# A quarter moved into the gated scan's weights, S5's powers taken jointly, and half of the memory's keys moved ahead of the merge

## The chip, the cores and the metric

The kernel runs on one core of a Trainium2 chip (trn2). The metric is the device time of one execution, in microseconds (us). A core has a matrix engine (TensorE, PE in the profile, with its weight loads shown as PEld), VectorE (DVE), ScalarE (ACT), GpSimd (POOL) and SyncE (SP), each with its own queue of instructions, and DMA engines that move weights from memory. An engine works through its queue in order, and waits where an instruction's data or buffer is not there.

## What is computed

The reference is a trunk of two decoder layers on 256 rows of 1024 channels, all in float32:

```
for l in range(DEPTH):
    h = rmsnorm(x, norm_mix[l])
    (u_ssm, q_lat, kv_lat, k_rope, hg_q, hg_f, hg_i, hg_g, gate_logits) = split(h @ w_in[l])
    y_ssm = s5_mixer(u_ssm, ...)     # diagonal complex scan, gelu, z_out * sigmoid(z_gate), [z_out, z_gate] = y @ w_glu
    y_mla = mla_mixer(q_lat, kv_lat, k_rope, ...)        # 8 causal heads
    y_hg  = hgrn2_mixer(hg_q, hg_f, hg_i, hg_g, lower_bounds[l], ...)  # gated linear recurrence, normed, gated, @ w_o
    gates = sigmoid(gate_logits).reshape(b, s, 3, 1024)
    merged = gates[..., 0, :] * y_ssm + gates[..., 1, :] * y_mla + gates[..., 2, :] * y_hg
    x = x + merged @ w_out[l]
    x = x + memory_cross_attention(rmsnorm(x, norm_cross[l]), rmsnorm(mem, norm_mem[l]), ...)  # k, v = split(mem @ w_kv)
    x = x + swiglu_ffn(rmsnorm(x, norm_ffn[l]), ...)
return rmsnorm(x, norm_final)
```

## The kernel before

**Weights.** All weight matrices stream once from memory. A `Chunk` is one transfer or two into one of `RB` = 3 raw buffers of 1 MB (tile `raw`), and is cut into units of up to 1024 columns. ScalarE copies a unit into a rounded high part `wH` (`acopy`, L232), and VectorE takes the rest, `wL` = raw - `wH` (`tt`, L221); there are `HU` = 4 buffers for each. PE multiplies three times per tile (all through `mm`, L213): high by high and high by low of the activations, and low by high. In `projA` (tiles `hv`, `quad`, `acc`, `dn`) that is one matmul of 512 columns with `wH` and one of 256 with `wL`; in `projB` (`gt`, `ho`, `mo`, `zg`, `zo`) it is three of 512.

**Stages of a layer.** The norm and the input projection (`quad`, `acc`, `hv`, then the gate logits `gt`, which give the gates `Tg`); beside these run tasks: S5 (`s5_powers`, `s5_main`), the recurrence `hgrn`, the attention `mla_attn` and the memory's norm `memory`. Then come the output projections of the three mixers (`ho`, `mo`, and `zg`, `zo` in `scan`), the merge's transposes (`mT`, split into `m`), `w_out` (`quad`, `hv`), cross attention and the FFN (`hv`, `dn`).

**S5.** `s5_powers` makes the operators: B times the powers 0 to 3 of the decay `lam` (`Q`), and C times its powers 0 to 4 (`Pw`, `P4`). `s5_main` works on two halves of 16 groups each: ScalarE masks `Q` into `Gp` and `Pw` into `Cp`, PE makes the scan's inputs (`gt<-ident,Gp`, `tm`, `b`), VectorE rotates (`w`), scans (`rt`), and rotates back into `X`, one for each of the real and the imaginary part; PE then forms `y` from `Cp` with `X` and from `Tm` with `Ush`.

**hgrn's output.** The squares of `o` are summed on PE (`oc<-ones,osq`), VectorE scales, GpSimd takes the power -1/2 (`s<-s,mhalf`, L250), PE spreads the result over the partitions (`ro<-ident,s`), VectorE multiplies (`osb<-osb,ro`), and the split gives `hox` for `ho`.

**The merge.** `scan(i)` handles half `i` of the output columns. `zg` is the gate of S5's output, `zo` its value; VectorE computes (tanh(zg/2)+1)*(g+1)/4*zo with g the tanh form of the merge gate, adds it to the accumulator `Tg` and PE transposes (`mT`). The sigmoids' factors are those quarters.

**The start.** `first(k)` feeds the first projection (`quad`) with `h` while ScalarE squares and GpSimd adds (`sq<-sq,sq`, L659; `fold`, L577) for the norm; `hg_bounds` computes the recurrence's lower bounds from `hg_lb` with small VectorE operations (`s`, 128x4).

**What sets the order.** The Python program emits the main line of projections, and `pace()` interleaves the tasks' steps with it by estimated engine times. SBUF tiles get slots from `plan` (class `Plan`, `SLOTS`), and the framework's scheduler then orders each engine's instructions by its own estimates, except where `tc.keep_in_program_order` pins one. Small edits so move instructions far from them.

## Time and profile before

| | us |
|---|---|
| runs before | 1093.49, 1093.5, 1094.94 |
| median of them | 1093.5 |
| the profiled execution's own time | 1094.6 |
| its span, first to last instruction | 1092.8 |
| PE busy in it | 1072.5 |
| VectorE busy | 829.1 |
| ScalarE busy | 636.4 |
| GpSimd busy | 37.7 |

The profiled execution is 1.1 us above the median. The busy time of an engine counts its instructions on data; PE's matmuls overlap, so that its rows can be longer than the distance to the next row. The mean granted clock of PE over the span is 0.992 of 2.4 GHz.

### The profile page before, as it was taken

The page shows a single profiled execution, that of the slowest core. Times are in us where ns is not written, and L with a number is a line of the kernel's source. Part 1 is how long each engine was busy: PE and PEld are TensorE (multiplying, and loading weights), DVE is VectorE, ACT ScalarE, POOL GpSimd, SP SyncE. Part 2 cuts the span into 40 slices and gives each one's busy share as a digit, 9 for nine tenths or more (in the row PEclk, how much of TensorE's full clock was granted, in tenths as well). Part 3 has the DMA queues.
Part 4 walks back from the last instruction along what each step waited for, and adds up shares of the span by engine and source line. Part 5 has one row for each costly group of instructions (what it writes and reads, how often), then busy time and mean ns, then how long its engine had stood idle before and what let it go on. Part 6 is the DMA issues. An engine that isn't in the chain of part 4 may idle for free.

```text
span 1092.8 us, 16654 instructions
## 1 busy us (share of the span) xinstructions
PE 1072.5 (98%) x6416; PEld 938.0 (86%) x6416; DVE 829.1 (76%) x1438; ACT 636.4 (58%) x1050; POOL 37.7 (3%) x52
## 2 busy tenths in 40 slices
PE   8999999989899999999999999999999999999997
PEld 8999888878688888888888899888888888888887
DVE  7996777786687789986768887767677868887753
ACT  6645756855455566564565447965545566555542
POOL 4001000000000000000010001000000000000000
PEclk9999999989899999999999999999999999999999
DMA  8745552342655455655656442543474535655551
GB/s 292 214 117 178 176 163 82 116 148 85 204 167 181 133 195 193 193 183 183 188 181 186 121 136 78 191 130 108 163 233 148 197 123 167 194 191 193 174 190 61
DMA packets 145024, 179.08 MB, mean 164 GB/s; under 512 B 13553, under 2 KB 108657, under 8 KB 144945
## 3 DMA queue, kind: packets, MB, share of 16 engines
q1 hardware_dynamic: 144512, 177.45, 50.6%
q8 instruction: 50, 0.82, 0.3%
q10 hardware_dynamic: 432, 0.57, 0.2%
q14 instruction: 30, 0.24, 0.1%
HBM read 174.59 MB, written 1.05 MB: 161 GB/s over the span
## 4 chain that ended last, share of the span: by engine, by line
PE 72%; ACT 1%; DVE 0%; issue 0%; POOLq 0%; POOL 0%; ACTq 0%
PE hv L213 32%; PE dn L213 11%; PE quad L213 6%; PE gt L213 6%; PE xv L213 2%; PE ho L213 1%; PE mo L213 1%; PE lv L213 1%; PE vps L213 1%; PE zg L213 1%; PE y L213 1%; PE zo L213 1%; PE xo L213 1%; PE b L213 1%; PE xS L213 1%; PE q L213 1%
## 5 line engine op out<-in xcount | busy, mean ns | idle before, releaser
L232 ACT ACTIVATE wH<-raw 128x1024 fp32r<-128x1024 f32 (+2 forms) x332 | 340.7, 1032 | 312.7 <-PE hv L213 81.3
L221 DVE TENSOR_TENSOR wL<-raw,wH 128x1024 fp32r<-128x1024 f32 (+2 forms) x332 | 394.8, 1192 | 158.2 <-ACT wH L232 152.1
L213 PE MATMUL hv<-h,wH 128*128 128x512 f32 x848 | 298.2, 396 | 0.0
L213 PE MATMUL hv<-h,wL 128*128 128x256 f32 x848 | 236.8, 282 | 0.0
L213 PEld LDWEIGHTS hv<-h,wH 128*128 128x128 f32 x848 | 158.6, 188 | 35.3 <-issue 0.2
L213 PEld LDWEIGHTS hv<-h,wL 128*128 128x128 f32 x848 | 160.4, 189 | 1.0
L213 PE MATMUL gt<-wH,h 128*128 128x512 f32 x384 | 123.6, 402 | 0.0
L213 PEld LDWEIGHTS gt<-wH,h 128*128 128x128 f32 x384 | 70.7, 188 | 13.4
L213 PE MATMUL gt<-wL,h 128*128 128x512 f32 x192 | 75.2, 397 | 0.2 <-DVE wL L221 0.2
L213 PE MATMUL dn<-dx,wH 128*128 128x512 f32 x176 | 61.6, 394 | 0.0
L213 PE MATMUL dn<-wH,dx 128*128 128x256 f32 (+1 forms) x264 | 58.7, 319 | 0.0
L213 PE MATMUL acc<-h,wH 128*128 128x256 f32 x288 | 52.5, 284 | 0.0
L213 PE MATMUL dn<-dx,wL 128*128 128x256 f32 x176 | 49.3, 280 | 0.0
L213 PEld LDWEIGHTS dn<-wH,dx 128*128 128x128 f32 x264 | 43.6, 189 | 4.0
L213 PE MATMUL quad<-h,wH 128*128 128x512 f32 (+1 forms) x160 | 44.6, 359 | 0.5 <-ACT wH L232 0.5
L213 PEld LDWEIGHTS acc<-h,wH 128*128 128x128 f32 x288 | 44.9, 192 | 0.1
L213 PEld LDWEIGHTS gt<-wL,h 128*128 128x128 f32 x192 | 35.9, 188 | 7.5 <-DVE wL L221 0.3
L213 PE MATMUL dn<-wL,dx 128*128 128x256 f32 (+1 forms) x132 | 41.9, 319 | 0.0
L213 PE MATMUL acc<-h,wL 128*128 128x256 f32 x144 | 40.8, 284 | 0.2 <-DVE wL L221 0.2
L213 PEld LDWEIGHTS dn<-dx,wH 128*128 128x128 f32 x176 | 33.1, 188 | 7.7
L213 PE MATMUL quad<-h,wL 128*128 128x256 f32 x128 | 33.8, 292 | 2.3 <-DVE wL L221 2.1
L213 PEld LDWEIGHTS dn<-dx,wL 128*128 128x128 f32 x176 | 33.1, 188 | 0.0
(375 smaller groups left out, 2017.4 us busy)
## 6 DMA issues: line engine op xcount, KB each, us to landing
raw<-in_w_in_dram SPq DMA_DIRECT2D x48, 1024.0 KB, 5.2
raw<-in_ffn_w_gate_up_dram SPq DMA_DIRECT2D x40, 1024.0 KB, 5.1
raw<-in_ffn_w_down_dram SPq DMA_DIRECT2D x17, 1024.0 KB, 5.2
raw<-in_ssm_w_glu_dram SPq DMA_DIRECT2D x16, 512.0 KB, 3.9
raw<-in_w_out_dram SPq DMA_DIRECT2D x8, 1024.0 KB, 7.3
raw<-in_x_w_kv_dram SPq DMA_DIRECT2D x8, 1024.0 KB, 5.1
raw<-in_ffn_w_down_dram SPq DMA_DIRECT2D x6, 768.0 KB, 4.8
raw<-in_hg_w_o_dram SPq DMA_DIRECT2D x4, 1024.0 KB, 5.1
```

Source lines behind the costliest of these rows:

```text
L213: return PE.matmul(o, l, r, start=start, stop=stop)
L221: DVE.tensor_tensor(out=o, in0=a, in1=b, op=op)
L232: return ACT.activation(out=o, in_=a, func=f, **kw)
```

## The change

Five edits. **(1)** In each layer the weights of `zg` and `zo` come as four chunks of 1 MB (rows of `w_glu` by two tiles, the gate's and the value's 512 columns behind one another) in place of eight of 512 KB, and their split multiplies by 0.25: ScalarE's copy by its scale, VectorE by a scalar_tensor_tensor (L217) in place of the tensor_tensor. The tanh of `zg` then needs no scale and VectorE's scaling of the gate, `ts(g_, g_, 0.25, 0.25, ...)`, falls away; (g+1)*zo and (u2+1)*that are two scalar_tensor_tensor. **(2)** `s5_powers` keeps `Q` and `Pw` in one tile `Z` of nine slots for each part, so that one power of both is one operation on 512 columns, where there were two on 256; the conjugate comes in through a sign (`sg_`). **(3)** `keys(0)`, half of the memory's keys (32 `hv<-ex` matmuls, with their chunk of `x_w_kv`), is emitted in `scan(1)` between the last `zo` and the transposes; before, all 64 stood behind `w_out`. **(4)** The column sums of the first norm (`ms`) are pinned between two steps of the first projection. **(5)** The first operation of `hg_bounds` is pinned to its place in the program.

```diff
-SLOTS = dict(t4=23, t2=10, t1=4, tn=8, tk=8, ps=8)
+SLOTS = dict(t9=2, t4=19, t2=10, t1=4, tn=8, tk=8, ps=8)
...
                 self.alloc(c.nk, h)
-                split(self.H, self.L, c.raw[:, :, h * j:h * j + h])
+                v = c.raw[:, :, h * j:h * j + h]
+                if c.quarter:
+                    acopy(self.H, v, scale=0.25)
+                    stt(self.L, v, 0.25, f(self.H), ALU.mult, ALU.subtract)
+                else:
+                    split(self.H, self.L, v)
...
                     for k in (0, 2):
-                        for n, c0 in (("zg", 1024), ("zo", 0)):
-                            C[n, i, k] = wcols(A["ssm_w_glu"][l], k, 2, c0 + 512 * i, 512, "one")
+                        C[part, i, k] = Chunk([wap(A["ssm_w_glu"][l], k, 2, c0 + 512 * i, 512) for c0 in (1024, 0)], 2, 1024)
+                        C[part, i, k].quarter = True
...
+        C["xk"] = [wcols(A["x_w_kv"][l], 0, 8, 0, 256)]
         C["wo"] = [wcols(A["w_out"][l], 4 * i, 4, 0, 512, "row") for i in range(2)]
         C["wo"] += [wcols(A["w_out"][l], 0, 8, 256 * i, 256) for i in range(2, 4)]
-        C["xk"] = [wcols(A["x_w_kv"][l], 0, 8, 256 * i, 256) for i in range(2)]
+        C["xk"].append(wcols(A["x_w_kv"][l], 0, 8, 256, 256))
...
             if j == 3:
                 fold(sq0[0], POOL)
+                nrm.sums = col_sums(sq0[0][:, 0], pin=True)
...
-        tt(lmx, gcol[:, lo:lo + 4], gcol[:, lo + 4:lo + 8], ALU.max)
+        tc.keep_in_program_order(tt(lmx, gcol[:, lo:lo + 4], gcol[:, lo + 4:lo + 8], ALU.max))
...
+        Z = [plan.tile(g, "t9", [128, 9, 16, 16], F32, nm("Z")) for n in range(2)]
+        S5Q[l] = Z
+        sg_ = tn([2, 16])
+        acopy(sg_[:, 0], lam[:, 1, ls])
+        acopy(sg_[:, 1], lam[:, 1, ls], scale=-1.0)
...
+        def cmul(o, a0, a1, b):
+
+            cm = [t2([512], F32, "cm")[:, 0:256 * o[0].shape[1]].rearrange("p (s i h) -> p s i h", i=16, h=16) for _ in range(4)]
+            tt(cm[0], a0, b[0], ALU.mult)
+            tt(cm[1], a1, b[1], ALU.mult)
+            tt(o[0], cm[0], cm[1], ALU.subtract)
+            tt(cm[2], a0, b[1], ALU.mult)
+            tt(cm[3], a1, b[0], ALU.mult)
+            tt(o[1], cm[2], cm[3], ALU.add)
...
+        cmul([z_[:, 3:4] for z_ in Z], bc(coef[:, 0, ls]), bc(coef[:, 1, ls]), [b_.unsqueeze(1) for b_ in B])
         yield
+        lr = lam[:, 0, ls].unsqueeze(1).unsqueeze(3).to_broadcast([128, 2, 16, 16])
         for k in range(1, 4):
-            cmul([q[:, 3 - k] for q in Q], lam, [q[:, 4 - k] for q in Q])
-            yield
...
-        for d in range(1, 5):
-            cmul([q[:, d] for q in Pw] if d < 4 else P4, lam, [q[:, d - 1] for q in Pw], conj=True)
-            yield
+            cmul([z_[:, 3 - k:5 + k:1 + 2 * k] for z_ in Z], lr, bc(sg_, 2), [z_[:, 4 - k:4 + k:2 * k - 1] for z_ in Z])
+            yield
+        cmul([z_[:, 8:9] for z_ in Z], bc(lam[:, 0, ls]), bc(sg_[:, 1]), [z_[:, 7:8] for z_ in Z])
...
-                    acopy(Cp[n][:, :, 0:3, g2, :].rearrange("p i k h -> p k i h"), Pw[n][:, 1:4, i0:i0 + 8, :], scale=gm[g2])
-                    acopy(Cp[n][:, :, 3, g2, :], P4[n][:, i0:i0 + 8, :], scale=gm[g2])
+                    acopy(Cp[n][:, :, :, g2, :].rearrange("p i k h -> p k i h"), Z[n][:, 5:9, i0:i0 + 8, :], scale=gm[g2])
...
-                act(u2[tt_], zg[tt_], AF.Tanh, scale=0.25)
-                g_ = Tg["s", i][:, tt_]
-                ts(g_, g_, 0.25, 0.25, ALU.mult, ALU.add)
-                stt(u2[tt_], u2[tt_], 1.0, g_, ALU.add, ALU.mult)
+                act(u2[tt_], zg[tt_], AF.Tanh)
             half("zo", zo, 2)
+            if i == 1:
+                drain()
+                keys(0)
             tps = [bank("mT") for _ in range(2)]
             for tt_ in range(2):
                 acc = Tg["h", i][:, tt_]
-                tt(u2[tt_], u2[tt_], zo[tt_], ALU.mult)
+                g_ = Tg["s", i][:, tt_]
+                stt(g_, g_, 1.0, zo[tt_], ALU.add, ALU.mult)
+                stt(u2[tt_], u2[tt_], 1.0, g_, ALU.add, ALU.mult)
                 tt(acc, acc, u2[tt_], ALU.add)
...
         drain()
-        Kc = t4([4, 256], F32, "Kc")
-        Rm = t1([256], F32, "Rm")
-        row_of(rmc, Rm)
-        for i in range(2):
-            kc = Kc[:, 2 * i:2 * i + 2]
-            add_up(kc, halves(C["xk"][i], ex))
-            tt(kc, kc, Rm.unsqueeze(1).to_broadcast([128, 2, 256]), ALU.mult)
+        keys(1)
```

The order of the instructions moves at places far from these lines too. VectorE's queue in the second half of S5 of layer 0, ahead of the first `X` (`w` are the rotated inputs, `cs` and `sn` cosine and sine, `rt` the scan's decay): before,

```order
L931 SCALAR_TENSOR_TENSOR w_2531<-rt_2346,w_2529 128x512
L221 TENSOR_TENSOR wL_2572<-raw_2279,wH_2571 128x1024
L221 TENSOR_TENSOR w_2528<-cs_2345,w_2530 128x8x63
L221 TENSOR_TENSOR s_2556<-s_2552,lsc_1283 128x2
L221 TENSOR_TENSOR w_2529<-sn_2344,w_2531 128x8x63
L228 TENSOR_SCALAR Tg_2596<-Tg_2596 128x512
L221 TENSOR_TENSOR wL_2732<-raw_2279,wH_2731 128x1024
L221 TENSOR_TENSOR X_2613<-w_2528,w_2529 128x8x63
```

and with the change:

```order
L937 SCALAR_TENSOR_TENSOR w_2445<-rt_2280,w_2443 128x512
L217 SCALAR_TENSOR_TENSOR ex_2859<-mT_2813,gcol,ex_2859 128x256
L221 TENSOR_TENSOR w_2443<-sn_2278,w_2445 128x8x63
L217 SCALAR_TENSOR_TENSOR ex_2859<-mT_2813,gcol,ex_2859 128x256
L217 SCALAR_TENSOR_TENSOR ex_2942<-mT_2813,gcol,ex_2942 128x256
L221 TENSOR_TENSOR X_2543<-w_2442,w_2443 128x8x63
```

Splits and gate scalings stood between the second scan and `X`; now three operations of the memory's norm (`ex`) stand there. A third split, before this excerpt, is gone from between `b` and `X` as well.

PE's queue at the end of the merge of layer 0: before,

```order
L213 MATMUL zo_2938<-wH_2941,yx_2701 128x512
L213 MATMUL zo_2938<-wL_2942,yx_2701 128x512
L1415 MATMUL mT_3024<-ident,Tg_1712 128x128 x2
L1415 MATMUL mT_3025<-ident,Tg_1712 128x128 x2
L213 MATMUL quad_3056<-m_1500,wH_2959 128x512
L213 MATMUL quad_3056<-m_1500,wL_2960 128x256
```

and with the change, from the last of the keys' matmuls on:

```order
L213 MATMUL hv_2983<-ex_2977,wH_2929 128x512
L213 MATMUL hv_2983<-ex_2977,wL_2930 128x256
L1420 MATMUL mT_3038<-ident,Tg_1675 128x128 x2
L213 MATMUL quad_3069<-m_1487,wH_2954 128x512
L213 MATMUL quad_3069<-m_1487,wL_2955 128x256
```

The transposes of the second half (`mT_3024` before, `mT_3038` now) followed the last `zo` directly. Now four `hv<-ex`, the eight transposes of the first half that remained, and 28 `hv<-ex` stand between.

PE's queue at hgrn's output in layer 0: before, behind the sums `oc` and 30 `gt`,

```order
L629 MATMUL ro_2010<-ident,s_1984 128x128 x4
L213 MATMUL gt_1884<-wH_1886,h_117 128x512
L213 MATMUL gt_1884<-wL_1887,h_117 128x512
L213 MATMUL S_2078<-Kh_1294,Qh_1292 128x128
L213 MATMUL gt_1885<-wL_1887,h_117 128x512
L213 MATMUL y_2166<-Tm_1904,Ush_333 64x4x32
L213 MATMUL y_2166<-Cp_2028,X_2062 64x4x32
```

and with the change, from the end of `y` on:

```order
L213 MATMUL y_1994<-Cp_1928,X_1949 64x4x32
L213 MATMUL oc_2019<-ones,osq_1963 128x1 x8
L213 MATMUL gt_1887<-wH_1888,h_117 128x512 x2
L213 MATMUL gt_1887<-wL_1889,h_117 128x512
L213 MATMUL S_2097<-Kh_1281,Qh_1279 128x128
L213 MATMUL S_2097<-Kh_1281,Qh_1279 128x256
L637 MATMUL ro_2065<-ident,s_2030 128x128 x4
L637 MATMUL ro_2083<-ident,s_2030 128x128 x4
L979 MATMUL yt_2054<-ident,ysh_2041 128x128 x4
L213 MATMUL S_2193<-Kh_1281,Qh_1279 128x128
L213 MATMUL S_2193<-Kh_1281,Qh_1279 128x256
L213 MATMUL ho_2091<-wH_1923,hox_2064 128x512
```

S5's `y` stood behind `ro`; now `oc`, `ro` and `ho` come behind `y`, close to one another.

## Rows read from the trace of the kernel before

**Rows 1.** The page, busy time and share of the span of an engine.

```profile
PE 1072.5 (98%) x6416; PEld 938.0 (86%) x6416; DVE 829.1 (76%) x1438; ACT 636.4 (58%) x1050; POOL 37.7 (3%) x52
```

**Rows 2.** Busy time by engine in stretches of 25 us, granted clock, DMA.

```profile
50.00:75.00 25.00, 25.00 (x182) 23.57 (x181) 24.97 (x75) 12.63 (x15) 0.00 (x0) 1.00 0.52 159
225.00:250.00 25.00, 21.15 (x122) 17.63 (x121) 20.11 (x43) 13.91 (x33) 0.92 (x3) 0.86 0.36 117
275.00:300.00 25.00, 21.18 (x97) 17.13 (x96) 15.87 (x24) 10.35 (x17) 0.00 (x0) 0.86 0.62 207
```

**Rows 3.** Timeline of PE: start, duration, instruction, idle time ahead and its releaser.

```profile
238.14 0.57 PE L213 MATMUL y<-Cp,X 128*64 128x128 f32 x2 [2.49 <-DVE X L221]
239.02 0.47 PE L1094 MATMUL PT<-ident,Ssb 128*128 128x128 f32 x1 [0.31 <-ACT Ssb L232]
240.55 0.69 PE L1094 MATMUL PT<-ident,Ssb 128*128 128x128 f32 x2 [1.05 <-DVE Ssb L226]
...
287.99 0.66 PE L1415 MATMUL mT<-ident,Tg 128*128 128x128 f32 x4 [2.36 <-DVE Tg L221]
...
290.81 0.77 PE L213 MATMUL quad<-m,wH 128*128 128x512 f32 x1 [1.46 <-DVE m L221]
```

**Rows 4.** Stretches of 1 us behind those pauses; the clock is third from the end.

```profile
244.00:245.00 1.00, 1.00 (x8) 1.00 (x9) 0.00 (x0) 1.00 (x5) 0.00 (x0) 0.50 0.00 0
295.00:296.00 1.00, 1.00 (x4) 0.81 (x4) 0.00 (x0) 0.00 (x0) 0.00 (x0) 0.50 0.01 1
```

**Rows 5.** Timeline of PE, ends of the two stretches at the lower clock.

```profile
241.17 0.69 PE L213 MATMUL y<-Cp,X 128*64 128x128 f32 x2
...
245.06 0.64 PE L213 MATMUL y<-Cp,X 128*64 128x128 f32 x6
...
296.52 0.40 PE L213 MATMUL quad<-m,wH 128*128 128x512 f32 x1
...
296.87 0.40 PE L213 MATMUL quad<-m,wH 128*128 128x512 f32 x1
```

**Rows 6.** Timelines of GpSimd, VectorE and PE, where GpSimd adds.

```profile
8.81 1.58 POOL L659 TENSOR_TENSOR sq<-sq,sq 128x512 f32<-128x512 f32 x1 [5.29 <-ACT sq L232]
...
91.86 0.74 POOL L577 TENSOR_TENSOR sqq<-sqq 128x256 f32<-128x256 f32 x1
...
9.13 1.28 DVE L221 TENSOR_TENSOR s<-s 128x4 f32<-128x4 f32 x1
...
91.90 1.24 DVE L221 TENSOR_TENSOR wL<-raw,wH 128x512 fp32r<-128x512 f32 x1 [0.89 <-ACT wH L232]
...
14.87 0.74 PE L213 MATMUL quad<-h,wL 128*128 128x256 f32 x4 [2.11 <-DVE wL L221]
```

**Rows 7.** Groups of VectorE's instructions: busy us and mean ns, idle before.

```profile
L221 DVE TENSOR_TENSOR wL<-raw,wH 128x1024 fp32r<-128x1024 f32 (+2 forms) x332 | 394.8, 1192 | 158.2 <-ACT wH L232 152.1
...
L221 DVE TENSOR_TENSOR cm<-lam,Pw 128x256 f32<-128x256 f32 x32 | 12.3, 419 | 0.1
...
L217 DVE SCALAR_TENSOR_TENSOR mu<-mu,Tg 128x512 f32<-128x512 f32 x8 | 5.5, 687 | 0.4 <-ACT mu L232 0.4
...
L228 DVE TENSOR_SCALAR Tg<-Tg 128x512 f32<-128x512 f32 x8 | 3.4, 423 | 1.6 <-ACT Tg L232 1.6
```

**Rows 8.** Timelines of GpSimd, PE and VectorE at hgrn's output (678.01 is layer 1).

```profile
170.22 2.48 POOL L250 TENSOR_TENSOR s<-s,mhalf 128x8 f32<-128x8 f32 x1 [5.14 <-DVE s L228]
...
678.01 1.64 POOL L250 TENSOR_TENSOR s<-s,mhalf 128x8 f32<-128x8 f32 x1 [13.54 <-DVE s L228]
...
175.86 1.03 PE L629 MATMUL ro<-ident,s 128*128 128x128 f32 x8
...
178.26 1.28 DVE L221 TENSOR_TENSOR osb<-osb,ro 128x512 f32<-128x512 f32 x2
...
181.58 1.28 DVE L221 TENSOR_TENSOR hox<-osb,hox 128x512 fp32r<-128x512 f32 x2
```

**Rows 9.** Timeline of PE behind the start.

```profile
29.99 0.39 PE L213 MATMUL acc<-h,wL 128*128 128x256 f32 x1 [0.23 <-DVE wL L221]
```

**Rows 10.** The page, DMA issues: KB each, median us from issue to landing.

```profile
raw<-in_w_out_dram SPq DMA_DIRECT2D x8, 1024.0 KB, 7.3
```

## What I predicted

> **What bounds the kernel now.** The page's first block says that TensorE (PE) is busy for 98% of the span [rows 1], so the time can fall by little more than PE's pauses, 20 us in all, and by work that PE does at its lower clock. I read PE in slices of 25 us. Nearly all slices are full of PE work, like 50 to 75 us; three are not: the first one (the start, before weights are there), 225 to 250 and 275 to 300 us, which hold 21.2 us each at a mean clock of 0.86 [rows 2]. The timeline of PE shows what stops it there. At 238.14 the S5 outputs `y` wait 2.49 us for VectorE's (DVE's) `X`, and at 240.55 the softmax transposes wait 1.05 for `Ssb`; a pause of 0.31 lies between. At 287.99 the merge's transposes `mT` wait 2.36 us for DVE's `Tg`, and at 290.81 `quad` waits 1.46 for `m` [rows 3]. Behind each pair of pauses the granted clock is 0.50, the 1.2 GHz level [rows 4]. From 241.17 to 245.06 the `y` matmuls [rows 5] run without a pause at that level, so about half of 3.9 us, 1.9, is lost. From 290.81 to 296.52 nine pairs of `quad` take 5.7 us; at full clock the next pair takes 0.35, nine would take 3.2, so 2.5 is lost [rows 3, 5]. Layer 1 has the same two places and no pause worth counting, so I expect nothing from it.
>
> **S5, second half of layer 0.** The wait at 238.14 is DVE's queue. Ahead of `X` stood three splits `wL` of 1.2 us each and two `Tg` scalings of 0.42 [rows 7]; the order of the change has none of these five between `b` and `X` and three `ex` operations on half as many columns instead, some 0.4 each: 4.4 us out, 1.2 in, so 3 us earlier. PE's cover grows too: 37 `gt` matmuls stand between the last `b` and the first `y`<-`X`, where 21 stood, at 0.23 each (512 of the 768 columns of a `quad` pair's 0.35) 3.7 us more. The wait was 2.5, so it goes, with margin: -3.85 (2.49 + 0.31 + 1.05) and, as the clock does not fall, -1.9. Sum **-5.75**. Both ends: nothing won if DVE comes to `b` 4 us late; no more than 5.75 can be won.
>
> **Merge of layer 0.** Before, after the last `zo`, DVE owed a product with `zo`, a sum, a split and the matching work of the other tile before PE could go on. Now 28 `hv<-ex` matmuls (14 pairs of 0.35 [rows 5], 4.9 us) stand between the transposes of the first half and those of the second, and four more ahead. What DVE owes in that time is four fused operations of 0.69 [rows 7], one split of 1.2 and a sum of 0.6 for the first tile; two splits of `m` and the other sum for the second: about 4.2 us for tile 0 and 5.6 for tile 1, needed at 6.5 (4 `hv`, 8 `mT`, 28 `hv`). So both waits (2.36 + 1.46) and the 2.5 of clock go: **-6.3**. Folding 0.25 into the weights costs nothing: ScalarE's copy has a scale anyway, and DVE's split is a scalar_tensor_tensor with as many columns (the group `mu<-mu,Tg` takes 0.69 for 512, as a tensor_tensor does); it removes four `Tg` scalings per layer, 1.7 us of DVE, hidden work elsewhere. The moved `hv` matmuls are the same in number; where they leave (behind `w_out`) 32 remain, and I see no DVE chain there longer than their 5.6 us.
>
> **Powers of S5.** 48 operations of 256 columns per layer become 12 of 256 and 18 of 512. At 0.42 (`cm`) and 0.69 a piece (the nearest row of that size) [rows 7] that is 20.2 against 17.5 us of DVE per layer, some 1 us of ScalarE per half for fewer `Cp` copies, and two small copies more. All of it lies at times when PE has no pause: 0 on the path, and -2.7 us at most if DVE's full stretch around 50 to 75 us had held PE up, which it did not.
>
> **The start.** `hg_bounds` leaves the first 15 us for 27 to 45 us. There its operations on 128x4 took 1.28 us, against some 0.15 elsewhere: the one at 9.13 began during GpSimd's addition of 8.81 (1.58 us) and ended with it [rows 6]. Three such are 3.4 us of DVE ahead of the `wL` for which PE waits 2.11 at 14.87, and there is about 1.3 of low clock behind it. A wait of the same kind meets a large split: `wL` of 128x512 at 91.90 took 1.24 beside GpSimd's fold at 91.86 [rows 6]. So the block belongs to whatever DVE issues while GpSimd adds; `h` or `wL` will stand in the queue instead, and I put the gain at 0 (ends: 0 and 3.4 + 1.3). The Trainium skill, "SBUF — State Buffer", "Who interferes with whom", says that a DVE instruction with two SBUF inputs contends with a GpSimd instruction that reads SBUF, and that issue order decides who blocks, for the whole instruction. By it, too, the start gains nothing; by the naive sum it gains up to 4.7.
>
> **What the change adds.** (a) Behind the start, `row` comes 24 `acc` matmuls later on PE, so the four `Ue` (on 256 columns, some 0.55 each) fall ahead of a split that `acc` needs; PE waited 0.23 for it at 29.99 [rows 9]. By laying the rows end to end I get 1.1, so **+0.9** (0 to 2.2, the four `Ue` in full). (b) The output of the gated scan `hgrn` in layer 0. Before, 30 `gt` matmuls (7 us) stood between the norm sums `oc` and their use `ro`, and `ro` did not wait, at 175.86 [rows 8]. Now `oc` stands behind all of `y`, with three `gt` and two `S` (1.1 us) ahead of `ro`. The chain in between is a small DVE operation and GpSimd's power, which took 2.48 and, in layer 1, 1.64 [rows 8]; with 1.64 PE waits about 1.0. Then `ho` needs `ro` times `osb` on DVE (0.6 each), a copy on ScalarE and the split `hox` (0.6 as well) [rows 8]; DVE has `ysh`, `ph` and a `wL` of 1.2 among them, PE has only `yt` and two `S` as cover: about 1.1 for the high part and 1.7 for the low. Together **+3.8** (0.5 if the power is short and `wL` early; 6 at the slow ends). (c) Both half-clock stretches above followed a pause over 2 us with more behind it; here the pauses are shorter but three, so the lower level costs 0 to 2.4; I take **+1.2**. (d) Four more table loads of ScalarE, 1.28 each, lie around 30 to 36 us on an engine that has pauses there: 0, or up to 2 if a weight copy behind them is late.
>
> **Sum.** -5.75 - 6.3 + 0.9 + 3.8 + 1.2 = -6.15. The profiled execution took 1094.6 (span 1092.8), 1.1 more than the median of 1093.5; from the median the forecast is **1087.3 us**. A measurement of this kernel tells about 0.2%, 2.2 us, from no change.
>
> **Rivals.**
> 1. The new waits at `ho` are covered (ScalarE's copy and DVE's split come while `ho` still has other weights) or the start does gain. Without (b) and (c) the time is 1082.3; with 2 of the start's 4.7 as well 1080.3. For it: before, `hox` and `ho` ran without a pause. Against it: the few matmuls between `oc`, `ro` and `ho`. Chance 0.28.
> 2. One of the two old pauses stays, because DVE reaches `b` or the last `zo` later than I laid it out: 5.75 or 6.3 come back, 1093.3. For it: I place DVE's start by PE's pace, and 2 us decide at the merge. Against it: at S5 chain and cover move the same way. Chance 0.15.
> 3. Slower: weights arrive late. The gate's weights now come as four chunks of 1 MB, each holding one of three raw buffers until both units are split, and the keys' chunk stands ahead of `w_out`. PE spends 24 matmuls, 5.6 us, on such a chunk; `w_out` took 7.3 us to land [rows 10]. If all four and the keys' chunk land at 7.9 apart, five waits of 2.3 make 11.5 and eat all that is won (11.2 net of (a)); at 8.5 the result is 3 to 4 us slower than before, 1097. Against it: two raw buffers ahead of use give over 10 us of lead, and the stretch 275 to 300 moved 207 GB/s, 5 us per MB [rows 2]. Chance 0.07.
> 4. The change does not do what it says, in that the added order only moves the waits by equal amounts (S5's into `hgrn`'s output, the merge's into `m`): within 2 us of 1093.5. Chance 0.07.
>
> My own case has 0.43, with a range of 1084.5 to 1090. To hold 8 in 10 the range goes from **1080.5** (rival 1 with part of the start) to **1093** (rival 2 in most of its width). Faster by over 0.2% is below 1091.3: all of my case and rival 1, a sixth of rival 2 and some of the others, without a little of my case's slow tail: 0.75. Within 0.2%: 0.17. Slower: 0.08.
>
> **What the profile after would show.** Right: no PE pause over 0.5 us ahead of the first `y`<-`X` of the second half and of `mT`; a clock of 1.00 in both stretches; at `ro` and `ho` of layer 0, around 175 to 185 us, pauses of 1 to 4 us in sum, ended by POOL or DVE; PE's busy time down by 2 to 4 us; the pause at 14.87 still near 2 us, with another DVE operation drawn out beside GpSimd. Wrong: a pause over 2 us at `X`, `Tg` or `m`; PE waiting on a DMA between `zg` and `quad`; or a new half-clock stretch that is longer than both old ones.

## The result, and the profile after

The changed kernel took 1080.28 us (median of four runs, 1080.19 to 1080.35), the kernel before 1093.95 beside it (1093.49 to 1094.94): 0.9874 of it, 95% interval 0.9857 to 0.9891. That is 13.7 us, more than twice the 6.15 that were forecast, and 0.2 us below the low end of the range. The profiled execution took 1080.19 (span 1078.4, 14.4 less than before's 1092.8), at a mean granted clock of 0.998.

The page's lines that answer to [rows 1] and [rows 10]: busy time of each engine, and one row of its DMA issues.

```profile
PE 1063.5 (99%) x6416; PEld 932.8 (86%) x6416; DVE 823.9 (76%) x1394; ACT 639.7 (59%) x1042; POOL 37.6 (3%) x52
...
raw<-in_w_out_dram SPq DMA_DIRECT2D x8, 1024.0 KB, 5.2
```

PE has the same 6416 matmuls and is busy for 9.0 us less, where 2 to 4 were forecast. Some 7.4 of that are matmuls that had run at the lower clock in this profile of before: 1.4 at the start, 3.5 at S5, 2.5 at the merge, worked out further down. `w_out` lands in 5.2 us, not 7.3.

Two of the stretches of 25 us of [rows 2], after:

```profile
225.00:250.00 25.00, 25.00 (x150) 21.22 (x150) 20.90 (x38) 15.24 (x30) 0.22 (x2) 1.00 0.48 146
275.00:300.00 25.00, 25.00 (x143) 21.70 (x142) 19.64 (x33) 13.86 (x22) 0.00 (x0) 1.00 0.57 187
```

Both of them, which stood out before, are now full, 25.00 against 21.15 and 21.18, at a clock of 1.00 against 0.86.

The timeline of the kernel after, at the places of [rows 3, 6, 8, 9] (start, duration, engine, instruction; in brackets the idle time ahead of it and what ended it):

```profile
8.53 1.36 POOL L667 TENSOR_TENSOR sq<-sq,sq 128x512 f32<-128x512 f32 x1 [5.01 <-ACT sq L232]
10.44 1.54 POOL L667 TENSOR_TENSOR sq<-sq,sq 128x512 f32<-128x512 f32 x1 [0.55 <-ACT sq L232]
12.28 1.74 POOL L667 TENSOR_TENSOR sq<-sq,sq 128x512 f32<-128x512 f32 x1 [0.29 <-ACT sq L232]
...
7.85 0.88 DVE L217 SCALAR_TENSOR_TENSOR h<-xp,gcol,h 128x256 fp32r<-128x256 f32 x2
10.36 1.91 DVE L217 SCALAR_TENSOR_TENSOR h<-xp,gcol,h 128x256 fp32r<-128x256 f32 x2
12.80 2.38 DVE L217 SCALAR_TENSOR_TENSOR h<-xp,gcol,h 128x256 fp32r<-128x256 f32 x2
...
12.93 0.74 PE L213 MATMUL quad<-h,wL 128*128 128x256 f32 x4 [0.73 <-DVE wL L221]
15.83 0.74 PE L213 MATMUL quad<-h,wL 128*128 128x256 f32 x4 [1.21 <-DVE wL L221]
28.67 0.38 PE L213 MATMUL acc<-h,wL 128*128 128x256 f32 x1 [1.15 <-DVE wL L221]
113.74 0.70 PE L213 MATMUL rope<-qraw,cf 128*128 128x256 f32 x2 [1.75 <-ACT qraw L232]
...
181.47 1.64 POOL L250 TENSOR_TENSOR s<-s,mhalf 128x8 f32<-128x8 f32 x1 [24.23 <-DVE s L228]
...
181.05 0.71 PE L213 MATMUL gt<-wH,h 128*128 128x512 f32 x2
...
181.82 0.82 PE L213 MATMUL S<-Kh,Qh 96*128 96x128 f32 x4
183.16 1.97 PE L637 MATMUL ro<-ident,s 128*128 128x128 f32 x8 [0.51 <-POOL s L250]
186.41 0.95 PE L213 MATMUL S<-Kh,Qh 96*128 96x128 f32 x4 [0.42 <-DVE osb L221]
188.81 0.50 PE L213 MATMUL ho<-wH,hox 128*128 128x512 f32 x1 [0.51 <-DVE hox L221]
...
234.85 0.68 DVE L221 TENSOR_TENSOR X<-w,w 128x504 f32<-128x504 f32 x1
238.10 0.38 PE L213 MATMUL y<-Cp,X 128*64 128x128 f32 x2
...
284.26 0.68 DVE L221 TENSOR_TENSOR Tg<-Tg,mu 128x512 f32<-128x512 f32 x1
286.36 0.38 PE L1420 MATMUL mT<-ident,Tg 128*128 128x128 f32 x2
```

**The two old waits are gone with margin.** `X` is done at 235.53, and the `y` that had waited 2.49 us for it starts at 238.10. The second `Tg` is done at 284.94, and its `mT`, which had waited 2.36, starts at 286.36. **The start:** PE's pauses there are 0.73 and 1.21, together 1.94, beside 2.11 before. While GpSimd adds, two `h` take 1.91 and 2.38 us, where two take 0.88 ahead of it. **hgrn's output:** 0.51, 0.42 and 0.51. **New:** 1.75 at `rope`, which no step of the prediction named. All pauses of PE's timeline make 13.85 before and 8.60 after. The "20 us in all" with which the prediction begins also held the 6.3 us behind PE's last matmul (1086.5 of 1092.8), which are no pause.

The granted clock (third from the end) in stretches of 1 us at hgrn's output, the only place of the kernel after, up to its last matmul, where it falls below 0.97:

```profile
183.00:184.00 1.00, 0.84 (x4) 0.84 (x5) 0.96 (x4) 1.00 (x3) 0.10 (x1) 0.54 0.00 0
184.00:185.00 1.00, 1.00 (x7) 1.00 (x6) 1.00 (x2) 0.56 (x1) 0.00 (x0) 0.50 0.00 0
185.00:186.00 1.00, 0.98 (x5) 0.58 (x3) 1.00 (x4) 0.00 (x0) 0.00 (x0) 0.50 0.00 0
186.00:187.00 1.00, 0.59 (x4) 0.57 (x5) 1.00 (x2) 0.98 (x3) 0.00 (x0) 0.76 0.00 0
```

Before, it fell in 16 to 20, 238 to 245 and 289 to 297.

### The profile page after: what moved, and what is told of

The parts are those of the page before. It is cut to its first block, busy times and chain, and to the rows that moved or that the text cites. A ratio compares the mean times of both kernels' runs of the same rounds, so it can differ in the third digit from the quotient of the medians.

```text
span 1078.4 us, 16592 instructions
## 1 busy us (share of the span) xinstructions
PE 1063.5 (99%) x6416; PEld 932.8 (86%) x6416; DVE 823.9 (76%) x1394; ACT 639.7 (59%) x1042; POOL 37.6 (3%) x52
## 4 chain that ended last, share of the span: by engine, by line
PE 96%; ACT 2%; DVE 1%; DMA 0%; issue 0%; POOLq 0%; POOL 0%; ACTq 0%
PE hv L213 33%; PE gt L213 12%; PE dn L213 11%; PE quad L213 7%; PE acc L213 5%; PE mo L213 2%; PE zo L213 2%; PE zg L213 2%; PE vps L213 2%; PE ho L213 2%; PE lv L213 2%; PE y L213 2%; PE xv L213 2%; PE b L213 1%; PE q L213 1%; PE oT L213 1%
## 5 line engine op out<-in xcount | busy, mean ns | idle before, releaser
L221 DVE TENSOR_TENSOR wL<-raw,wH 128x1024 fp32r<-128x1024 f32 (+2 forms) x316 | 375.2, 1191 | 152.7 <-ACT wH L232 149.1
```

The costliest lines, as they stand in the source:

```text
L221: return DVE.tensor_tensor(out=o, in0=a, in1=b, op=op)
```

## The experiments

Theory A: each edit acts through the pause that the prediction names, so that the sum of the terms holds and only sizes are off. Theory B: something else in the change gave most of it, such as weights that come earlier, the start, or the clock. The runs do one edit alone on the kernel before, then leave one out of the whole, then test single terms. Kernels that were measured together share their runs of before. Those of different groups ran on different chips, so between groups the ratios are compared.

### One edit alone

**e1_keys**, edit (3):

```diff
+            if i == 1:
+                drain()
+                keys(0)
             tps = [bank("mT") for _ in range(2)]
```

> Only the move of half the memory's keys, on the kernel before. PE's queue has 32 hv<-ex between the last zo and the merge's transposes in both layers; S5, hgrn and the start stand as before. Theory A (each edit removes the waits of its own place, and the gains add): both waits at the merge of layer 0 go (2.36 + 1.46) with the 2.5 us of lower clock behind them, layer 1 gives 0.5 to 1 as well; the waits at X in S5 stay: 1093.5 - 6.3 - 0.7 = about 1086.5. Theory B (the merge gains only if DVE's chain is shortened by the quarter too): DVE still owes the product, the sums and a split per tile, so a wait of 1 to 2 us at mT or m stays, with its clock: 1089 to 1091.

1085.87 us (1084.75 to 1087.89), ratio 0.993 [0.991, 0.995]. No pause is left at `mT` and `m`; `X` still waits 2.49. The keys alone remove the merge's waits, as Theory A has it.

**e2_powers**, edit (2), of which one line is shown:

```diff
-            cmul([q[:, 3 - k] for q in Q], lam, [q[:, 4 - k] for q in Q])
+            cmul([z_[:, 3 - k:5 + k:1 + 2 * k] for z_ in Z], lr, bc(sg_, 2), [z_[:, 4 - k:4 + k:2 * k - 1] for z_ in Z])
```

> Only the joint powers of S5, on the kernel before. The order of S5 and hgrn in layer 0 becomes that of the whole change (39 matmuls between the last b and the first y<-Cp,X where 21 stood, 3 between oc and ro where 30 stood). Theory A: all of S5's gain comes from this edit, by the order that it brings and not by the 2.7 us of DVE per layer: 5.75 won at X, 1.5 to 3 lost at ro, ho and in the clock behind, 1 to 2 won in the FFN and layer 1: 1088 to 1090; the two waits at the merge stay. Theory B: the two Tg scalings that the quarter removes are needed too, a wait of 0.5 to 1 stays at X: 1090 to 1092. If the FFN between 390 and 495 us gets 0.7 shorter here, that part belongs to the powers as well.

1090.83 us (1088.04 to 1091.37), ratio 0.9973 [0.9961, 0.9986]. The pause at `X` is gone, and the ones at hgrn's output (0.52, 1.58, 0.21) and at `rope` (1.77) are there: the powers set the order of S5 and hgrn, and bring both the gain and the price. `quad` waits 1.74 and 3.26 for `m`. The mechanism is Theory A's, since no wait is left at `X`; the time is in Theory B's range.

**e3_quarter**, edit (1), scale and chunks:

```diff
+                if c.quarter:
+                    acopy(self.H, v, scale=0.25)
+                    stt(self.L, v, 0.25, f(self.H), ALU.mult, ALU.subtract)
...
+                        C[part, i, k] = Chunk([wap(A["ssm_w_glu"][l], k, 2, c0 + 512 * i, 512) for c0 in (1024, 0)], 2, 1024)
+                        C[part, i, k].quarter = True
```

> Only the quarter in the weights of zg and zo and their chunks of 1 MB, on the kernel before. Two Tg scalings leave DVE's queue ahead of X in the second half of S5 (0.34 each as it steps): X comes 0.7 earlier, the wait there falls from 2.49 to 1.8. At the merge the transposes still follow the last zo directly, and DVE owes four operations of 0.69 and two sums there in place of two and two. Theory A (no cover, no gain): the wait at mT stays 2 to 4 us, total 1092 to 1094. Theory B (the fused form shortens DVE's chain enough): the merge's waits fall by half or more, 1089 to 1091.

1089.01 us (1088.1 to 1090.7), ratio 0.9962 [0.9945, 0.9979]. `X` waits 1.82 instead of 2.49 (0.67 less, near the 0.84 of the two `Tg` scalings that are gone), `mT` 1.10, `m` 1.41. The time is Theory B's, though the merge's waits fell by a third and not by half.

**e4_pins**, edits (4) and (5):

```diff
-        if l == 0:
-            nrm.sums = col_sums(sq0[0][:, 0])
...
+                nrm.sums = col_sums(sq0[0][:, 0], pin=True)
...
+        tc.keep_in_program_order(tt(lmx, gcol[:, lo:lo + 4], gcol[:, lo + 4:lo + 8], ALU.max))
```

> Only the two pins (column sums of the first norm, first operation of the recurrence's bounds), on the kernel before. The start becomes that of the whole change: no 128x4 operation ahead of the first splits, row 24 acc matmuls later. Theory A (the trace of the whole change: quad ends 2.2 earlier, 0.9 lost again at acc): 1092.2, the clock in 16 to 20 us stays at full level, although DVE's operations are drawn out beside GpSimd's additions as before. Theory B (what I forecast: the block only meets another instruction, and the start gives nothing): 1093.5 to 1094.5 with the loss at acc.

1093.05 us (1088.29 to 1095.37), ratio 0.9998 [0.9986, 1.0009]. The start's pauses are 0.70 and 1.22, `acc` waits 1.14: what the pins give at the start, the later `row` takes at `acc`. The time lies between the two theories, and the interval holds no change.

The four medians are 7.5, 2.5, 4.4 and 0.3 below before's 1093.37, 14.7 in sum; the whole has 13.1 in its second measurement (e9_whole). The sums agree to within 2 us, but the single gains are not what the same edits are worth within the whole (see e10 to e12).

### The halves of the quarter

**e5_chunks** has the chunks of 1 MB without the 0.25, **e6_scale** the 0.25 on chunks of 512 KB:

```diff
-                        for n, c0 in (("zg", 1024), ("zo", 0)):
-                            C[n, i, k] = wcols(A["ssm_w_glu"][l], k, 2, c0 + 512 * i, 512, "one")
+                        C[part, i, k] = Chunk([wap(A["ssm_w_glu"][l], k, 2, c0 + 512 * i, 512) for c0 in (1024, 0)], 2, 1024)
```

```diff
-                split(self.H, self.L, c.raw)
+                if c.quarter:
+                    acopy(self.H, c.raw, scale=0.25)
+                    stt(self.L, c.raw, 0.25, f(self.H), ALU.mult, ALU.subtract)
...
-                tt(u2[tt_], u2[tt_], zo[tt_], ALU.mult)
+                g_ = Tg["s", i][:, tt_]
+                stt(g_, g_, 1.0, zo[tt_], ALU.add, ALU.mult)
+                stt(u2[tt_], u2[tt_], 1.0, g_, ALU.add, ALU.mult)
```

> Of the quarter's edit only the chunks: the gate's weights in four chunks of 1 MB, split as before, no 0.25 in them, the Tg scalings stay; on the kernel before. Theory A (lead): with three raw buffers a chunk of 512 KB gives half the lead, and ScalarE's waits on raw<-ssm_w_glu and raw<-w_out around 268 to 282 us (4.5 and 3.9 before, none in the run of the quarter) came from that; they vanish here too, DVE's splits come earlier, mT and m wait about 2.5 in sum where it was 3.8, X stays at 2.49: 1089.5 to 1091. Theory B (the gain of the quarter is DVE's work): the waits stay, 1093.

> Of the quarter's edit only the 0.25 in the weights and the fused DVE form, with the chunks of 512 KB as before. Theory A (lead): ScalarE's DMA waits of 4 us stay, the waits at mT and m stay at 3 to 4, only X falls from 2.49 to 1.8: 1092 to 1093. Theory B (DVE's work): 1089 to 1090, as with the whole edit.

e5_chunks: 1090.14 us (1089.25 to 1091.45), ratio 0.9971 [0.9959, 0.9983]. e6_scale: 1092.6 (1088.77 to 1093.07), ratio 0.9982 [0.9968, 0.9997]. What the chunks do stands on ScalarE. Its timeline in the kernel before, where the gate's weights are split:

```profile
270.55 1.06 ACT L232 ACTIVATE wH<-raw 128x1024 fp32r<-128x1024 f32 x1 [4.48 <-DMA raw<-in_ssm_w_glu_dram]
...
280.34 2.01 ACT L232 ACTIVATE wH<-raw 128x1024 fp32r<-128x1024 f32 x2 [3.87 <-DMA raw<-in_w_out_dram]
```

and in e6_scale, ScalarE and PE:

```profile
269.71 1.06 ACT L232 ACTIVATE wH<-raw 128x1024 fp32r<-128x1024 f32 x1 [4.58 <-DMA raw<-in_ssm_w_glu_dram]
...
276.52 1.06 ACT L232 ACTIVATE wH<-raw 128x1024 fp32r<-128x1024 f32 x1 [2.84 <-DMA raw<-in_ssm_w_glu_dram]
...
280.02 2.01 ACT L232 ACTIVATE wH<-raw 128x1024 fp32r<-128x1024 f32 x2 [2.44 <-DMA raw<-in_w_out_dram]
...
287.78 1.12 PE L1419 MATMUL mT<-ident,Tg 128*128 128x128 f32 x4 [3.10 <-DVE Tg L221]
```

For comparison e4_pins, which also has chunks of 512 KB:

```profile
276.53 1.06 ACT L232 ACTIVATE wH<-raw 128x1024 fp32r<-128x1024 f32 x1 [1.65 <-DMA raw<-in_w_out_dram]
...
284.36 0.66 PE L1416 MATMUL mT<-ident,Tg 128*128 128x128 f32 x4 [0.74 <-DVE Tg L221]
```

In e5_chunks, e3_quarter and the whole ScalarE waits for no DMA there. A raw buffer holds 1 MB, and three are in the ring; a 512 KB chunk takes a whole one, so that the weights on their way are half as much work. The late copies make late splits on DVE, and these stand in the queue ahead of `Tg`: with the scale alone `mT` waits longer (3.10) than before (2.36), with the chunks alone 0.74. How late the weights of the 512 KB chunks are differs between executions: in the profile of e4_pins `w_out` keeps ScalarE waiting for 1.65 instead of 3.87, and `mT` waits 0.74 there too. So the wait at `mT` in a single profile doesn't show what the chunks do on PE. It is shown by ScalarE, which waits for the gate's weights in all six profiles with chunks of 512 KB and in none of the ten with 1 MB, and by the ten runs of e5_chunks at 0.9971. Chunks of 1 MB bring weights earlier, as Theory A has it for e5 and e6. Rival 3 looked at the right place, the arrival of the gate's weights, with the wrong sign.

### Single terms

**e7_no_ms_pin**, the whole with the column sums back at their old place:

```diff
-                nrm.sums = col_sums(sq0[0][:, 0], pin=True)
...
+        if l == 0:
+            nrm.sums = col_sums(sq0[0][:, 0])
```

> The whole change without the pin of the first norm's column sums (the pin of the recurrence's bounds stays). PE's row comes after 2 acc matmuls again, not 24. Theory A (the late row puts four Ue ahead of acc's split): the pause of 1.15 at acc falls to 0.2, so that the time is 0.9 below the whole change, 1079.4; S5 has 48 matmuls of cover where it had 37, no pause there. Theory B (the pin also shields the first projection from a pause): quad ends later by what acc gains, 1080 to 1081.

1083.12 us (1080.41 to 1084.93), ratio 0.9906 [0.9888, 0.9925]: `acc` waits 0.46 instead of 1.15, but `rope` 2.38 and `ho` 1.16. The later `row` costs its 0.7, and yet the kernel with it is 2.9 faster by the medians, and 1.6 by the ratios of this run and e9_whole, whose intervals overlap; both theories missed that. Without the pin the order differs at two places far behind, and this profile has the clock at 0.50 behind its longer pause at `rope` and behind `ro`. The one run of the six at a mean clock of 0.998 took 1080.41, as the whole does, so the difference is in the main lower clock.

**e8_ro_early**, e7_no_ms_pin with S5's `y` of layer 0 held back until hgrn's sums are emitted, to give `ro` its cover:

```diff
+            while l == 0 and hf == 0 and "ro" not in HGD:
+                yield
...
+        HGD.append("ro")
```

> As e7_no_ms_pin, and in layer 0 S5's y of the first half is emitted only when hgrn has emitted its norm sums: PE has oc within the y matmuls, five eighths of them ahead of ro. Theory A (the waits at hgrn's output are the chain oc, DVE, GpSimd, ro without cover): the pause of 0.51 at ro goes, one of 0.5 to 1.5 at ho stays (DVE multiplies, ScalarE copies, no cover), the clock stays at full level more often there: 1 to 2 less than e7, 1077.5 to 1078.5. Theory B (ho's pause takes all of it): same as e7 within 0.5.

1084.87 us (1084.53 to 1086.32), ratio 0.9926 [0.9909, 0.9943]. No pause at `ro`, but 3.04 at `ho`, which waits for `hox`. The wait moved one step along the chain; the chain from `oc` to `ho` is what counts, not `ro`. The time is 1.75 above e7_no_ms_pin, outside both theories.

**e9_whole**, the changed kernel again, with no edit.

> The whole change once more, on the same chip as the next three, because times of one kernel differ between chips by where the clock falls. Pauses as in its first trace: 0.7 and 1.2 at the start, 1.15 at acc, 0.5, 0.4 and 0.5 at hgrn's output, none at X, mT, m: 1079.5 to 1082. If e7_no_ms_pin was slower than this only by its chip, this run lies at 1082 to 1084.

1080.24 us (1080.22 to 1080.38), ratio 0.9891 [0.987, 0.9912]. This profile shows no stretch at the lower clock at hgrn's output. PE's timeline there:

```profile
183.33 1.09 PE L637 MATMUL ro<-ident,s 128*128 128x128 f32 x8 [0.51 <-POOL s L250]
184.71 0.66 PE L979 MATMUL yt<-ident,ysh 128*128 128x128 f32 x4 [0.29 <-DVE ysh L217]
186.58 0.92 PE L213 MATMUL S<-Kh,Qh 96*128 96x128 f32 x4 [1.21 <-DVE osb L221]
188.98 0.50 PE L213 MATMUL ho<-wH,hox 128*128 128x512 f32 x1 [0.56 <-DVE hox L221]
```

The pauses are 2.57 in sum, 1.13 more than the 1.44 of the first profile, and `ro` takes 1.09 instead of 1.97. From the first `vps` (a projection that starts at 45.80 and 45.98 us) to the first `xS` of the cross attention both executions take 281.55 us. PE waited there for GpSimd and VectorE, whose instructions kept their durations (`osb` takes 0.68 at 185.00 in the first profile, where PE's clock is 0.50, and at 185.17 in this one), and in the time of its slower work it would have waited anyway. The run is not on e7_no_ms_pin's chip, so it doesn't settle what that chip does; the medians of before on the two are 1093.7 and 1093.36.

### The whole without one edit

**e10_no_powers**, **e11_no_quarter** and **e12_no_keys**, a few lines of each edit:

```diff
-            cmul([z_[:, 3 - k:5 + k:1 + 2 * k] for z_ in Z], lr, bc(sg_, 2), [z_[:, 4 - k:4 + k:2 * k - 1] for z_ in Z])
+            cmul([q[:, 3 - k] for q in Q], lam, [q[:, 4 - k] for q in Q])
```

```diff
-                        C[part, i, k] = Chunk([wap(A["ssm_w_glu"][l], k, 2, c0 + 512 * i, 512) for c0 in (1024, 0)], 2, 1024)
-                        C[part, i, k].quarter = True
```

```diff
-            if i == 1:
-                drain()
-                keys(0)
```

> The whole change without the joint powers. Theory A (gains of the parts add; the powers alone gave 2.95): 3 slower than the whole. X waits 1.8 to 1.9 in the second half of S5 of layer 0 (the quarter takes the Tg scalings away), Ssb 0.5 and 1.2, and nothing at hgrn's output. Theory B (the powers only exchange S5's pauses for those at hgrn's output): within 1 of the whole.

> The whole change without the quarter and its chunks of 1 MB. Theory A (gains add; the quarter alone gave 4.15): 4 slower than the whole. Theory B (the keys' cover at the merge already hides what the quarter saved there: both act on the same two pauses): ScalarE waits 3 to 4 us for raw<-ssm_w_glu again, but PE does not at mT or m; 0 to 1.5 slower than the whole.

> The whole change without the moved keys. Theory A (gains add; the keys alone gave 7.6): 7 slower than the whole. Theory B (the quarter has taken a part of the same pauses): mT and m wait about 1.1 and 1.4 as with the quarter alone, with the clock behind them: 4 to 5.5 slower than the whole.

| | us (range) | ratio [95%] | above e9_whole |
|---|---|---|---|
| e10_no_powers | 1084.64 (1083.82 to 1085.08) | 0.993 [0.9911, 0.9949] | 4.4 |
| e11_no_quarter | 1082.52 (1081.84 to 1084.24) | 0.9913 [0.9893, 0.9932] | 2.3 |
| e12_no_keys | 1084.53 (1083.23 to 1085.03) | 0.9929 [0.9911, 0.9947] | 4.3 |

PE's timeline in e10_no_powers, second half of S5, layer 0:

```profile
236.33 0.41 PE L213 MATMUL y<-Cp,X 128*64 128x128 f32 x2 [1.82 <-DVE X L221]
237.21 0.47 PE L1103 MATMUL PT<-ident,Ssb 128*128 128x128 f32 x1 [0.48 <-ACT Ssb L232]
238.74 0.69 PE L1103 MATMUL PT<-ident,Ssb 128*128 128x128 f32 x2 [1.05 <-DVE Ssb L226]
```

and in e12_no_keys, at the merge:

```profile
283.54 0.63 PE L213 MATMUL quad<-m,wH 128*128 128x512 f32 x1 [2.58 <-DVE m L221]
```

Each old pause comes back with its edit: without the powers the three at S5 (and none at `ro`, `ho` or `rope`), without the keys one at the merge, with the clock low from 283.8 to 287.2 behind it. Without the quarter `mT` waits 0.89, `mo` 0.59, and ScalarE waits 1.19, 1.93 and 1.69 us for the gate's weights.

So the places are shown, but the gains don't add. Powers, quarter and keys are worth 2.5, 4.4 and 7.5 alone and 4.4, 2.3 and 4.3 when left out of the whole. The keys came out in Theory B's range (the quarter has taken a part of their pauses), the powers above Theory A's 3, the quarter between its two theories. That the single gains made nearly the whole's 13.1 is in part that these differences cancel.

### The start, and the new pause

**e13_qraw**, the whole with a higher priority for the copy that `rope` waits for:

```diff
-            acopy(qraw, pp[:, 0:256])
+            with tc.high_priority(offset=400):
+                acopy(qraw, pp[:, 0:256])
```

> The whole change, with ScalarE's two copies `qraw` given a higher priority, so that in layer 0 the first of them stands ahead of the two `Kh` copies (2.0 us) instead of behind them; downstream, two `S` matmuls move from ahead of `ho` to behind its first four. If the new pause at `rope` (1.75 us at 113.74 in the profile after) is ScalarE's queue and is lost time, it shrinks by most of 1.75, and the time falls by about that from the whole's 1080.3, to 1078.4 to 1079.2, if the moved `S` does not cost as much at `ho` (0.2 each). Rival: the pause is only where PE's lead over the other engines is taken back; then it moves to a later instruction, and the time stays within 0.4 of 1080.3.

1083.05 us (1081.81 to 1086.52), ratio 0.9921 [0.9895, 0.9946]. All four runs are slower than every run of the whole, by 1.4 to 6.3 us, on another chip. ScalarE's and PE's timelines:

```profile
111.23 0.36 ACT L232 ACTIVATE qraw<-qp 128x256 f32<-128x256 f32 x1
111.62 2.00 ACT L232 ACTIVATE Kh<-kraw 32x1024 f32<-32x1024 f32 x2
...
114.27 1.04 ACT L232 ACTIVATE wH<-raw 128x1024 fp32r<-128x1024 f32 x1
...
115.37 0.73 PE L213 MATMUL gt<-wH,h 128*128 128x512 f32 x2 [1.51 <-ACT wH L232]
...
187.10 1.24 PE L213 MATMUL ho<-wH,hox 128*128 128x512 f32 x4 [2.59 <-ACT hox L232]
```

The rival's mechanism holds, its time (within 0.4) doesn't. `rope` no longer waits, but 1.51 us come back at `gt`, which needs the weight copy that stands behind the same `Kh`. What PE waits for is the whole of ScalarE's queue from 107.7 to 115 us (copies of `Gp`, a table load of 1.28, `sn`, `Kh`), and it hardly matters which instruction shows it. At `ho`, which lost the two `S` as cover, the pause is 2.59, where `S` and `ho` had 1.21 and 0.56 in e9. All pauses make 9.49 us, beside 9.43 in e9, so they only moved; the 1.6 us that this profiled execution is longer lie at hgrn's output, with the clock at 0.50 from 188.1 to 191.5. Why the median is 2.8 above the whole's is not shown.

**e14_no_hg_pin**, the whole without edit (5):

```diff
-        tc.keep_in_program_order(tt(lmx, gcol[:, lo:lo + 4], gcol[:, lo + 4:lo + 8], ALU.max))
+        tt(lmx, gcol[:, lo:lo + 4], gcol[:, lo + 4:lo + 8], ALU.max)
```

> The whole change without the pin of `hg_bounds`: its small VectorE operations stand in the start again. If, as the prediction said, GpSimd's block then only falls on them in place of `h` and `wL`, the start's pauses stay near 2 us in sum and the time within 0.7 of the whole's 1080.3. Rival: the pin is what gave the start's 2.2 us in the profiles; then PE comes to the first `acc` about 2 us later and the time is 1081.5 to 1083.

1080.92 us (1080.83 to 1082.76), ratio 0.9895 [0.9878, 0.9911]; 0.7 above the whole by the medians, 0.4 by the ratios. PE's timeline of the start:

```profile
14.80 0.74 PE L213 MATMUL quad<-h,wL 128*128 128x256 f32 x4 [2.10 <-DVE wL L221]
...
29.44 0.39 PE L213 MATMUL acc<-h,wL 128*128 128x256 f32 x1 [1.07 <-DVE wL L221]
```

Its pause is the one of before, 2.10 beside 2.11, and yet PE comes to the first `acc` 1.39 us sooner than before. One stretch of 1 us tells why, first in the kernel before, then in e14_no_hg_pin, then in e1_keys, which has the start of before as well:

```profile
17.00:18.00 1.00, 1.00 (x6) 1.00 (x7) 1.00 (x3) 0.46 (x1) 0.00 (x0) 0.50 1.06 345
```

```profile
17.00:18.00 1.00, 1.00 (x11) 1.00 (x10) 1.00 (x3) 0.48 (x1) 0.00 (x0) 1.00 1.01 353
```

```profile
17.00:18.00 1.00, 1.00 (x7) 1.00 (x6) 1.00 (x3) 0.50 (x1) 0.00 (x0) 0.50 1.02 354
```

At 0.50 PE has 6 matmuls in that microsecond, at 1.00 it has 11. Behind the same pause of 2.1 us the clock fell in some profiles and not in others: of the seven that have the old start it fell in four (before, e1_keys, e5_chunks, e6_scale) and not in e2_powers, e3_quarter and e14. In none of the nine profiles with `hg_bounds` pinned, where the pauses are 0.5 to 0.8 and 1.2, did it fall there. So the pin gave 0.7 to 0.9 without the clock, and in this pair of profiles 1.4 more through it. That the pin prevents the fall is likely by these counts, and not shown.

## Why the prediction was wrong

The profile's difference of 14.4 us by the prediction's terms. A group's time is the distance from one PE row's start to the next, without the pauses, which are counted apart.

| term | forecast | measured | of which pauses |
|---|---|---|---|
| up to 47 us (start, (a)) | +0.9 | -1.3 | +0.7 |
| S5, second half, layer 0 | -5.75 | -7.4 | -3.85 |
| merge of layer 0 | -6.3 | -6.6 | -3.8 |
| hgrn's output, (b) and (c) | +5.0 | +3.25 | +1.2 |
| `rope` | 0 | +1.6 | +1.6 |
| the rest of layer 0 to cross attention | 0 | -1.2 | 0 |
| from there to the end | 0 | -2.7 | -1.1 |
| sum | -6.15 | -14.4 | |

**S5 and the merge: right.** The places, the direction and the pauses came out as forecast (e1, e10 and e12 show which edit does which). The failed size is the clock at S5: the forecast counted 1.9 for the `y` from 241.17 on. The matmuls that ran below full clock from 238 on were `y` (2.20 gained), `PT` (0.78) and `oT` (0.56), 3.5. At the merge 2.5 was forecast for `quad` and 2.54 measured.

**"Together +3.8" and "+1.2" at hgrn's output: mis-sized.** The pauses came where they were put, with 1.44 after and 2.57 in e9 against 3.8. All in all this place cost 3.25, not 5.0. At `ro` 0.51, not 1.0: the GpSimd power took the 1.64 that was assumed, but the three `gt` and the `S` ahead of `ro` cover 1.6 us (181.05 to 182.64), not 1.1. At `S` and `ho` 0.4 and 0.5 in place of 1.1 and 1.7 at `ho`. The clock did fall (to 0.50 for three microseconds), and by e9 that cost nothing net: slower work replaced waiting. Here a term for low clock beside a term for waits in the same microseconds counted the same time twice.

**"I put the gain at 0" for the start: right about the block, wrong about the clock.** The block moved to `h` (1.91 and 2.38 for two, 0.88 without GpSimd). The Trainium skill, "SBUF — State Buffer", section "Who interferes with whom", says that a VectorE instruction with two SBUF inputs contends with a GpSimd instruction that reads SBUF, and that the order of issue decides which of them is blocked; the rows agree. The start's pauses fell by 0.17 only. The pin's 0.7 to 0.9 (e14) stands against the later `row`'s 0.9, and (a) measured 1.15 - 0.23 = 0.92, as forecast. The remaining -1.4 is the clock: the prediction saw "about 1.3 of low clock" behind the old pause and put it at 0 with the rest, and the clock fell in four of seven profiles of the old start and in none of nine of the new one.

**The zeros: wrong.** "Layer 1 has the same two places and no pause worth counting, so I expect nothing from it": its merge is 1.1 us shorter, and its pauses of 0.31 and 0.30 there and of 0.47 at `o` are gone. Keys alone shorten that merge (from its first `zg` to the first `xS`) by 1.4, the scale alone by 1.1, the chunks alone by 0.2. For the powers, "0 on the path": e2 and the whole spend 0.7 to 0.8 us less in layer 0's FFN, where no other edit does. This is no scatter: the FFN's 593 `hv` matmuls take 104.21 us from the first to the last (390.83 to 495.04 before) in each of the seven profiles without the joint powers and 103.50 (379.06 to 482.56 after) in each of the nine with them. PE has no pause there in either; the steps from one matmul to the next are shorter, by 0.2 to 0.3 us in a hundred behind the first 300. The edit changes VectorE's work there (the powers of layer 1) and the slots of the tiles (`SLOTS`); which of the two does it was not tested. The -1.2 in the rest of layer 0 is spread in the same way, over `tm` (0.45), `lv` (0.41), `o` (0.33) and `x` (0.20), and no run singles out its cause. And `rope` is the same zero with the other sign, +1.6: ScalarE's work of S5's first half now stands ahead of `qraw`. It comes with the powers (e2, e9, e11, e12) and is absent without them (e1, e3 to e6, e10).

**The failing steps.** The pauses at the two old places (3.85 and 3.82) went as forecast. Of the 8.2 us that the sum missed in this pair of profiles, 4.2 are its terms for the lower clock: 1.9 at S5 where 3.5 was gained, 0 at the start where 1.4 was, and +1.2 at hgrn's output that cost nothing net. The second failing step is the zeros for the rest of the kernel: 3.9 were gained there (the rest of layer 0, its FFN, layer 1), of which `rope`, another zero, took 1.6 back. The price on the waits of the new order was near: 3.25 for 3.8. The rest are the pin's 0.85 and 0.3 at the merge.

Of the rivals, the first named a time (1080.3 to 1082.3) next to the result. Its conditions came half: the start did gain about 2 in the profiles, 1.4 of it by the clock, but at hgrn's output 3.25 of the 5.0 that it leaves out stayed, and gains that it doesn't name made up for them. That its time is so near is luck in part. The third had chunks of 1 MB make weights late; they made them early, worth some 3 us alone by e5. Its argument counted the bytes that a chunk holds and not the lead that a ring of three gives when each buffer is full.

**What the clock adds.** In 61 runs of the kernel before beside the experiments the time goes with the granted clock: 1088.69 and 1088.70 at 0.998, 1096.06 to 1096.28 at 0.989. All eight runs of the changed kernel have 0.998 or 0.999 and agree within 0.2 us. At equal mean clock the change is thus worth 8.4 us, and some 5 of the 13.7 are lower-clock stretches that the kernel before has in most executions and the changed one has not, or has where they cost nothing. What is open: why the clock falls behind a given pause in one execution and not in the next, and why the matmuls of layer 0's FFN follow one another a little faster.

## What to carry to other kernels

When an order is remade by a scheduler, price the places far from the edit too: here they held +3.25, +1.6 and -3.9 us beside the two pauses that the change removed, and 1.4 us of clock at the start came and went between profiles of the same instructions, so that a gain by the clock has to be counted over several executions. Count PE's low clock only where PE is not waiting for another engine in the same microseconds. Don't add the gains of single edits where two of them act on the same pause. In a ring of few buffers of fixed size, chunks that half fill a buffer halve the prefetch lead, and here the engine that copies them showed it first, with waits of 4.48 and 3.87 us for DMA from 266 us on, some 20 us ahead of PE's first wait there.

## What the runs showed of the hardware

The lower level of the clock (1.2 GHz, 0.50 in the rows) also came without a pause of PE ahead of it. In e1_keys no row of PE between 155 and 175 us has a wait; these are its rows ahead of the fall and its clock:

```profile
164.51 1.67 PE L213 MATMUL b<-Ush,G 128*128 128x64 f32 x14
166.02 1.00 PE L213 MATMUL oc<-ones,osq 128*128 128x1 f32 x8
...
167.89 0.95 PE L213 MATMUL oc<-ones,osq 128*128 128x1 f32 x8
```

```profile
168.00:169.00 1.00, 1.00 (x10) 0.98 (x9) 1.00 (x3) 1.00 (x3) 0.00 (x0) 0.96 0.00 0
169.00:170.00 1.00, 1.00 (x4) 0.73 (x3) 1.00 (x3) 0.44 (x1) 0.02 (x1) 0.50 0.00 0
```

PE counts as busy for the whole microsecond. Ahead of the fall it ran 14 matmuls of 64 columns, 16 of one column and four `gt` of 512 between these. The same instructions stand at this place in before and in e3 to e6 and e10; in e5_chunks the clock fell there too (at 168.7), and in the other five profiles it stayed at 1.00. In the kernel after, `oc` also stands ahead of the fall at 183.1, but there with the pause of 0.51 between. A PE that is busy throughout was thus no assurance of the clock here, and what makes one execution lose it is not shown.
